# Routing of a top-16 expert layer: candidate rows of eight, and keys found in float16 pairs

## The chip, the cores and the metric

One NeuronCore of a Trainium2 chip runs the whole program; the other seven are idle. The metric is the device time of one execution in microseconds (us), and the kernel before has a median of 2887.47 us over 3 runs (2885.11 to 2893.48). The engines are named as the profile names them: PE (matmul), PEld (weight load), DVE (vector), ACT (scalar), POOL (GpSimd, here the source of gather DMAs), SP (the queue that issues the other DMAs).

## The reference, cut to what matters

The model is two layers. Each has an attention mixer and then a PEER layer: per token and head, two lists of 128 key scores are cut to their best 16, the 16 x 16 sums of the two lists are cut to the best 16, and each of these names one of 16384 experts.

```python
q = (t @ w_q).reshape(b * n, PEER_HEADS, 2, PEER_KEY_DIM)      # 8 heads
s = jnp.einsum('thcd,hcnd->thcn', q, sub_keys)                 # 128 scores per list
sv, si = lax.top_k(s, PEER_TOPK)                               # 16 best of each list
cand = (sv[:, :, 0, :, None] + sv[:, :, 1, None, :]).reshape(b * n, PEER_HEADS, 256)
score, pos = lax.top_k(cand, PEER_TOPK)
i1 = jnp.take_along_axis(si[:, :, 0], pos // PEER_TOPK, axis=-1)
i2 = jnp.take_along_axis(si[:, :, 1], pos % PEER_TOPK, axis=-1)
expert = i1 * PEER_KEYS + i2
gate = jax.nn.softmax(score.astype(jnp.float32), axis=-1)
# then, per token: sum over the 128 chosen experts of gate * gelu(t . u[expert]) * v[expert]
```

Layer 0 does this for 512 tokens (256 of context, 256 of the sequence), layer 1 for the 256 of the sequence.

## The kernel before, in words

A PEER layer computes most tokens densely: a first pass runs over 128 blocks of the table u, and a block multiplies 128 experts with all dense tokens (8 tiles of 128 inputs, and for each three matmuls, since each number is carried as a high and a low float32r part). A second pass does the same with v, after the gelu has been multiplied by a dense weight matrix. The last 128 tokens of layer 0 and the last 32 of layer 1 are done in another way: their experts' rows of u and v are gathered, one row per partition, by POOL's indirect DMA (`fetch`), and DVE multiplies and adds them ("rows", `rows_u` and `rows_v`). So layer 0 has 384 dense tokens and layer 1 has 224.

The routing of a layer runs beside its first pass, in `route`. It has three parts. First 16 steps, one for each head and list: 24 matmuls for the query, a copy by ACT, a score matmul per tile of 128 tokens, and on DVE the 16 best of each list (`top16`: two MAX8, three searches). Then, for each tile of 128 tokens, the sums of the two lists that can be among the best 16 (50 of them, in seven groups `RUNS`), `top16` over these for each of 8 heads, and a one-hot search that finds the expert's number of each chosen place: for two heads at a time a comparison of 2 x 16 x 50 elements with the place (`eq`), a product with the expert numbers, and a sum, all float32 on DVE. The tile with the gathered tokens comes first. Last, `weights`: PE transposes first key, second key and gate of the tile (into `pt`), ACT and DVE copy them as `idx`, and for every 8 tokens DVE makes four one-hot arrays in float16 (tiles `kth`, `ktl`, `qth`, `qtl`), PE multiplies them (32 matmuls of 128 columns), ACT copies the result, and SP writes it to memory (`wd`).

`peer` calls `route` as a generator: each `yield` names a share of work, and after each block of u the routing advances until its sum of shares reaches `(b + 1) * rate`. So the shares and the rate set where the routing's instructions are written between the blocks. The final order on each engine is then made by the tile framework's scheduler before the run, from its own estimates; on the chip each engine runs its list in that order and waits where an input is not there. Two things bend this order. The split of each block of u into high and low part (`split_to`: ACT's cast into `wh`, DVE's subtraction into `wl`, three buffers each) has high priority. And the rows on DVE are held in order behind each other and behind the latest split (`row`, `behind`).

The lines that the change touches are in `route`, the numbers `RUNS` and `NCAND`, one constant tile (`iota`) and the `rate` in `peer`. `self.keys` (named `iota` in the profile, as is the float32 one) holds 0 to 127 in float16, each number twice. In the profile, L990, L993 and L995 are the one-hot search, L963 the sums, L924 to L928 `top16`, L1008 to L1011 the chain that splits an expert's number into its two keys (tiles `ei`, `ef`), L1013 to L1015 the transposes, L1040 to L1043 the one-hot arrays of `weights`, L157 and L158 the two halves of a split, L1121 a row of u, L1098 its gather.

Of the kernel before, what the change touches and what calls it, by code (L numbers as in the profile page):

```python
# [29 lines left out]
PH, TOPK, NK = 8, 16, 128  # L30
# [7 lines left out]
ROUTE_END, LAST = 118, 3  # L38
# [4 lines left out]
RUNS = ((0, 1, 16), (1, 2, 8), (2, 3, 5), (3, 4, 4), (4, 5, 3), (5, 8, 2), (8, 16, 1))  # L43
NCAND = 50
# [82 lines left out]
class Kernel:  # L127
# [125 lines left out]
    def consts(self):  # L253
        nc = self.nc
        jp = self.t([128, 128], I32, "cv")
        nc.gpsimd.iota(jp, pattern=[[1, 128]], base=0, channel_multiplier=-1)
        self.ident = self.t([128, 128], F, "ident")
        nc.vector.tensor_scalar(self.ident, jp, 0.0, None, op0=OP.is_equal)
        self.ones = self.t([128, 128], F, "ones")
        nc.vector.memset(self.ones, 1.0)  # L260
        self.iota = self.t([128, NCAND], F, "iota")
        nc.gpsimd.iota(self.iota, pattern=[[1, NCAND]], base=0, channel_multiplier=0,
                       allow_small_or_imprecise_dtypes=True)
# [666 lines left out]
    def route(self, layer, hh, hl, T, n):  # L930


        nc, a = self.nc, self.a
        nt = T // 128
        sv = self.t([128, nt, 8, 2, TOPK], F, "vh", 2)
        si = self.t([128, nt, 8, 2, TOPK], U32, "vh", 2)
        for hc in range(16):
# [14 lines left out]
            yield 1.0  # L952
        sf = self.t([128, nt, 8, 2, TOPK], F, "vl", 2)
        nc.vector.tensor_copy(sf, si)
        nc.vector.tensor_scalar(sf[:, :, :, 0], sf[:, :, :, 0], 128.0, None, op0=OP.mult)
        for tt in [nt - 1] + list(range(nt - 1)):
            cand = self.t([128, 8, NCAND], F, "kh", 2)
            ec = self.t([128, 8, NCAND], F, "kh", 2)
            o = 0
            for a0, a1, nb in RUNS:  # L960
                na = a1 - a0
                for dst, src in ((cand, sv), (ec, sf)):
                    nc.vector.tensor_tensor(dst[:, :, o:o + na * nb].rearrange("p h (a b) -> p h a b", a=na),  # L963
                                            src[:, tt, :, 0, a0:a1, None].to_broadcast([128, 8, na, nb]),
                                            src[:, tt, :, 1, None, 0:nb].to_broadcast([128, 8, na, nb]), op=OP.add)
                o += na * nb
            yield 1.8
            cv = self.t([128, 8, TOPK], F, "cv")
            cp = self.t([128, 8, TOPK], U32, "cp")
            c2 = self.t([128, 8, NCAND], F, "s2", 5)  # L970
            for h in range(8):
                self.top16(cv[:, h], cp[:, h], cand[:, h], c2[:, h])
                if h % 2:
                    yield 1.2
# [4 lines left out]
            nc.scalar.activation(cv, cv, AF.Exp)  # L979
            nc.vector.tensor_reduce(z, cv, axis=AX, op=OP.add)  # L980
# [3 lines left out]
            cf = self.t([128, 8, TOPK], F, "cf")  # L984
            nc.vector.tensor_copy(cf, cp)
            e = self.t([128, 8, TOPK], F, "e")
# [10 lines left out]
            fl = [x.rearrange("p h j -> p (h j)") for x in (e, cv)]  # L997
            nd = 128
            if tt == nt - 1:
                nd = 128 - n  # L1000
                self.rows_routed(layer, n, *fl)
                self.routed = True
                yield 1.0
            if not nd:
                continue
            ei = self.t([128, 2, 128], I32, "ei")
            ef = self.t([128, 2, 128], F, "ef")
# [7 lines left out]
            nc.tensor.transpose(pT[:, 2], fl[1], self.ident)  # L1015
# [5 lines left out]
            yield 1.8  # L1021
# [120 lines left out]
    def peer(self, layer, hh, hl, T, n, tags, finish, aside=iter(())):  # L1142
# [12 lines left out]
        rate = (16 + T // 128 * 30 + Td / 8 * 2.4) / ROUTE_END  # L1155
# [190 lines left out]
```

## Time and profile before

| | us |
|---|---|
| median of 3 runs | 2887.47 |
| the profiled execution | 2880.45 |
| its span, first to last instruction | 2878.7 |
| PE busy | 2641.1 (92%) |
| DVE busy | 2345.1 (81%) |
| ACT busy | 1271.4 (44%) |
| POOL busy | 492.7 (17%) |

The first pass of layer 0 lies at about 393 to 1093 us of the span, its second pass at 1093 to 1720, the mixer of layer 1 up to about 2000, the first pass of layer 1 at about 2010 to 2505, the second pass to the end. Busy shares are averages over these; a stage has to be looked at by itself. The granted clock of PE has two levels here, 2.4 GHz (1.00) and 1.2 GHz (0.50), and a stretch in between is a mixture.

### The profile page before, as it was taken

The page shows a single profiled execution, that of the slowest core. Times are in us where ns is not written, and L with a number is a line of the kernel's source. Part 1 is how long each engine was busy: PE and PEld are TensorE (multiplying, and loading weights), DVE is VectorE, ACT ScalarE, POOL GpSimd, SP SyncE. Part 2 cuts the span into 40 slices and gives each one's busy share as a digit, 9 for nine tenths or more (in the row PEclk, how much of TensorE's full clock was granted, in tenths as well). Part 3 has the DMA queues.
Part 4 walks back from the last instruction along what each step waited for, and adds up shares of the span by engine and source line. Part 5 has one row for each costly group of instructions (what it writes and reads, how often), then busy time and mean ns, then how long its engine had stood idle before and what let it go on. Part 6 is the DMA issues. An engine that isn't in the chain of part 4 may idle for free. (4 is left out here: it accounts for less than half of the span.)

```text
span 2878.7 us, 44735 instructions
## 1 busy us (share of the span) xinstructions
PE 2641.1 (92%) x16487; PEld 2458.7 (85%) x16487; DVE 2345.1 (81%) x4838; ACT 1271.4 (44%) x1989; POOL 492.7 (17%) x417
## 2 busy tenths in 40 slices
PE   8999989989989899999899998987879899899998
PEld 4788778988979899988899897756879799889998
DVE  7989887998989886978889757876786968668887
ACT  3468532335445453332233333363333556545553
POOL 0113200033323332322333200020000011101000
PEclk9999989999999999999999998968989799999999
DMA  6420433489989899998899854604436699979995
GB/s 225 128 92 16 154 131 110 164 288 317 324 298 338 297 372 332 373 337 318 323 341 387 318 174 137 208 16 139 146 127 238 221 335 316 336 288 357 352 355 170
DMA packets 285278, 712.47 MB, mean 247 GB/s; under 512 B 30209, under 2 KB 130177, under 8 KB 282881
## 3 DMA queue, kind: packets, MB, share of 16 engines
q1 hardware_dynamic: 238978, 541.81, 53.5%
q0 software_dynamic: 46080, 167.79, 16.4%
q8 instruction: 129, 2.11, 0.3%
q14 instruction: 91, 0.75, 0.1%
HBM read 626.64 MB, written 82.84 MB: 246 GB/s over the span
## 5 line engine op out<-in xcount | busy, mean ns | idle before, releaser
L157 ACT CAST wh<-wr 128x1024 fp32r<-128x1024 f32 (+1 forms) x361 | 375.9, 1042 | 813.3 <-PE pa L205 328.9
L158 DVE TENSOR_TENSOR wl<-wr,wh 128x1024 fp32r<-128x1024 f32 (+1 forms) x361 | 436.2, 1209 | 140.2 <-ACT wh L157 139.1
L206 PE MATMUL pa<-A,wl 128*128 128x384 f32 (+1 forms) x1216 | 425.8, 351 | 8.9 <-DVE wl L158 8.9
L205 PE MATMUL pa<-C,wh 128*128 128x384 f32 (+2 forms) x1224 | 427.7, 350 | 0.0
L204 PE MATMUL pa<-A,wh 128*128 128x384 f32 (+1 forms) x1216 | 426.3, 352 | 0.9 <-ACT wh L157 0.9
L206 PE MATMUL pa<-B,wl 128*128 128x224 f32 (+3 forms) x1288 | 379.5, 295 | 41.3 <-DVE wl L158 41.0
L204 PE MATMUL pa<-B,wh 128*128 128x224 f32 (+3 forms) x1288 | 380.3, 297 | 8.5 <-ACT B L404 4.3
L205 PE MATMUL pa<-B,wh 128*128 128x224 f32 (+1 forms) x1216 | 349.9, 288 | 0.2
L206 PEld LDWEIGHTS pa<-B,wl 128*128 128x128 f32 (+1 forms) x1288 | 260.3, 202 | 47.6 <-DVE wl L158 44.0
L1098 POOL DMA_INDIRECT B<-urow,cg x128 | 178.2, 1392 | 557.5 <-DVE B L1121 309.8
L204 PEld LDWEIGHTS pa<-B,wh 128*128 128x128 f32 (+1 forms) x1288 | 260.0, 202 | 14.4 <-ACT B L404 5.1
L157 ACT CAST wh<-pT 128x1024 fp32r<-128x1024 f32 x144 | 151.1, 1050 | 234.0 <-PE pa L205 228.6
L206 PEld LDWEIGHTS pa<-A,wl 128*128 128x128 f32 x1216 | 232.4, 191 | 20.0 <-DVE wl L158 11.8
L205 PEld LDWEIGHTS pa<-B,wh 128*128 128x128 f32 x1216 | 247.0, 203 | 1.2 <-issue 0.5
L205 PEld LDWEIGHTS pa<-C,wh 128*128 128x128 f32 (+1 forms) x1224 | 233.9, 191 | 8.9 <-DVE C L405 0.5
L204 PEld LDWEIGHTS pa<-A,wh 128*128 128x128 f32 x1216 | 232.5, 191 | 9.8 <-ACT wh L157 1.2
L158 DVE TENSOR_TENSOR wl<-pT,wh 128x1024 fp32r<-128x1024 f32 x144 | 175.6, 1221 | 69.7 <-ACT wh L157 68.3
L205 PE MATMUL pa<-pT,wh 128*128 128x384 f32 x512 | 178.7, 349 | 35.2 <-DVE pT L158 34.9
L1121 DVE SCALAR_TENSOR_TENSOR B<-B 128x1024 f32<-128x1024 f32 x128 | 155.4, 1217 | 33.3 <-DMA B<-urow,cg 32.6
L1247 PE MATMUL pa<-pT,wh 128*128 128x448 f32 x512 | 171.5, 378 | 7.1 <-DVE pT L158 4.5
L206 PE MATMUL pa<-pT,wl 128*128 128x384 f32 x512 | 175.5, 343 | 0.0
L204 PE MATMUL pa<-pT,wh 128*128 128x384 f32 x512 | 175.1, 343 | 0.0
(379 smaller groups left out, 6527.3 us busy)
## 6 DMA issues: line engine op xcount, KB each, us to landing
wr<-v SPq DMA_DIRECT2D x152, 512.0 KB
wr<-u SPq DMA_DIRECT2D x128, 512.0 KB
pT<-u SPq DMA_DIRECT2D x128, 512.0 KB
wd<-c SPq DMA_DIRECT2D x38, 1024.0 KB
B<-v SPq DMA_DIRECT2D x72, 512.0 KB
gd<-px SPq DMA_DIRECT2D x64, 384.0 KB
px<-gd SPq DMA_DIRECT2D x63, 384.0 KB
q<-adaw SPq DMA_DIRECT2D x38, 512.0 KB
```

What stands on the lines that cost most here:

```text
L157: nc.scalar.copy(hi, src)
L158: return nc.vector.tensor_tensor(lo, src, hi.bitcast(F), op=OP.subtract)
L204: nc.tensor.matmul(out, lhs[0], rhs[0], start=start, stop=False, **kw)
L205: nc.tensor.matmul(out, lhs[0], rhs[1], start=False, stop=False, **kw)
L206: nc.tensor.matmul(out, lhs[1], rhs[0], start=False, stop=stop, **kw)
L1098: f = self.nc.gpsimd.indirect_dma_start(out=g, out_offset=None, in_=table, in_offset=bass.IndirectOffsetOnAxis(ap=self.eid[:, j:j + 1], ax ...
L1121: self.row(nc.vector.scalar_tensor_tensor(g, g, 1.0, self.own, op0=OP.mult, op1=OP.mult, accum_out=self.act[:, j:j + 1]))
L1247: nc.tensor.matmul(acc[j][:, :2 * Td], v[0][:, s], aa, start=bb == 0, stop=False, skip_group_check=True)
```

## The change

Candidates: instead of 50 sums in seven groups of different width, 80 in ten rows of eight. Rows 0 and 1 are the first entry of the first list with all 16 of the second, rows 2 to 8 are entries 1 to 7 with the first eight, row 9 is entries 8 to 15 with the first one. Row and column of a chosen place are then its number shifted by 3 and its last three bits, and a few operations on 128 elements turn them into the two list positions. The sums are made for four heads at a time, three instructions each.

Keys: for each of the two lists the position is compared with 0 to 15 (not the place with 0 to 49), in float16 and in pairs, for all 8 heads in one instruction of 2048 elements; then the product with the list of keys, and four additions that halve the row each time. The float32 array of expert numbers (`ec`) is gone; the lists are cast once per layer to float16, each entry twice. The two keys come out apart, so the chain L1008 to L1011 is gone; for the gathered tile one instruction joins them.

Shares and rate: the 16 steps count 0.6 instead of 1.0, a tile counts about 20 instead of 30, and the rate follows.

```diff
-NCAND = 50
+NCAND = 80
-            yield 1.0
-        sf = self.t([128, nt, 8, 2, TOPK], F, "vl", 2)
-        nc.vector.tensor_copy(sf, si)
-        nc.vector.tensor_scalar(sf[:, :, :, 0], sf[:, :, :, 0], 128.0, None, op0=OP.mult)
+            yield 0.6
+        lists = self.t([128, nt * 256, 2], H, "vl", 2)
+        nc.vector.tensor_copy(lists, si.rearrange("p t h s j -> p (t h s j)")[:, :, None].to_broadcast([128, nt * 256, 2]))
+        lists = lists.rearrange("p (t h s j) b -> p t h s (j b)", t=nt, h=8, s=2)
+        yield 1.0
...
+            for h0 in (0, 4):
+                cand = self.t([128, 4, NCAND], F, "kh", 2)
+                hs = slice(h0, h0 + 4)
+                for o, a0, na, nb in ((0, 0, 1, 16), (16, 1, 7, 8), (72, 8, 8, 1)):
+                    sh = [128, 4, na, nb]
+                    nc.vector.tensor_tensor(cand[:, :, o:o + na * nb].rearrange("p h (a b) -> p h a b", a=na),
+                                            sv[:, tt, hs, 0, a0:a0 + na, None].to_broadcast(sh),
+                                            sv[:, tt, hs, 1, None, 0:nb].to_broadcast(sh), op=OP.add)
+                c2 = self.t([128, 4, NCAND], F, "s2", 5)
+                for h in range(4):
+                    self.top16(cv[:, h0 + h], cp[:, h0 + h], cand[:, h], c2[:, h])
+                    if h % 2:
+                        yield 2.1
...
+            nc.vector.tensor_scalar(rc[:, 0], fcp.bitcast(I32), 3, None, op0=OP.logical_shift_right)
+            nc.vector.tensor_scalar(rc[:, 1], fcp.bitcast(I32), 7, None, op0=OP.bitwise_and)
+            nc.vector.tensor_copy(rf, rc)
+            r, c = rf[:, 0], rf[:, 1]
...
+            nc.vector.scalar_tensor_tensor(m, r, 9.0, c, op0=OP.is_equal, op1=OP.mult)
+            nc.vector.tensor_tensor(c, c, m, op=OP.subtract)
+            nc.vector.tensor_scalar(ab[:, 0], r, -1.0, 0.0, op0=OP.add, op1=OP.max)
+            nc.vector.tensor_tensor(ab[:, 0], ab[:, 0], m, op=OP.add)
+            nc.vector.tensor_scalar(ab[:, 1], r, 1.0, 8.0, op0=OP.is_equal, op1=OP.mult)
+            nc.vector.tensor_tensor(ab[:, 1], ab[:, 1], c, op=OP.add)
+            yield 2.0
...
-            for h in range(0, 8, 2):
-                eq = self.t([128, 2, TOPK, NCAND], F, "q", 4)
-                sh = [128, 2, TOPK, NCAND]
-                nc.vector.tensor_tensor(eq, self.iota[:, None, None, :].to_broadcast(sh),
-                                        cf[:, h:h + 2, :, None].to_broadcast(sh), op=OP.is_equal)
-                yield 1.75
-                nc.vector.tensor_tensor(eq, eq, ec[:, h:h + 2, None, :].to_broadcast(sh), op=OP.mult)
-                yield 1.75
-                nc.vector.tensor_reduce(e[:, h:h + 2], eq, axis=AX, op=OP.add)
-                yield 1.7
+            ef = self.t([128, 2, 128], F, "ef")
+            for i in range(2):
+                eq = self.t([128, 64, 16, 2], H, "q", 4)
+                nc.vector.tensor_tensor(eq, self.keys[:, None, 0:16].to_broadcast([128, 64, 16, 2]),
+                                        ab[:, i].rearrange("p (g b) -> p g b", b=2)[:, :, None].to_broadcast([128, 64, 16, 2]),
+                                        op=OP.is_equal)
+                yield 1.3
+                e8 = eq.rearrange("p (h k) j b -> p h k (j b)", h=8)
+                nc.vector.tensor_tensor(e8, e8, lists[:, tt, :, i, None].to_broadcast([128, 8, 8, 32]), op=OP.mult)
+                yield 1.3
+                e1 = eq.rearrange("p g j b -> p g (j b)")
+                for w in (16, 8, 4):
+                    nc.vector.tensor_tensor(e1[:, :, 0:w], e1[:, :, 0:w], e1[:, :, w:2 * w], op=OP.add)
+                nc.vector.tensor_tensor(ef[:, i].rearrange("p (g b) -> p g b", b=2), e1[:, :, 0:2], e1[:, :, 2:4], op=OP.add)
+                yield 1.4
...
-            nc.vector.tensor_copy(ei[:, 0], fl[0])
-            nc.vector.tensor_scalar(ei[:, 1], ei[:, 0], 127, None, op0=OP.bitwise_and)
-            nc.vector.tensor_scalar(ei[:, 0], ei[:, 0], 7, None, op0=OP.logical_shift_right)
-            nc.vector.tensor_copy(ef, ei)
...
-        rate = (16 + T // 128 * 30 + Td / 8 * 2.4) / ROUTE_END
+        rate = (16 * 0.6 + T // 128 * 20 + Td / 8 * 2.4) / ROUTE_END
```

The change also moves instructions. The first place is on DVE in layer 0, at the end of the search for the first dense tile: `ef` are the two keys that PE transposes, `B,rg` is a row of u, `wl` a split. Before:

```order
L158 TENSOR_TENSOR wl<-pT,wh 128x1024
L1008 CAST ei<-e 128x128
L1121 SCALAR_TENSOR_TENSOR B,rg<-B 128x1024
L1009 TENSOR_SCALAR ei<-ei 128x128
L1121 SCALAR_TENSOR_TENSOR B,rg<-B 128x1024
L158 TENSOR_TENSOR wl<-pT,wh 128x1024
L1010 TENSOR_SCALAR ei<-ei 128x128
L1121 SCALAR_TENSOR_TENSOR B,rg<-B 128x1024
L1011 CAST ef<-ei 128x256
L1121 SCALAR_TENSOR_TENSOR B,rg<-B 128x1024
L158 TENSOR_TENSOR wl<-wr,wh 128x1024
L1020 SCALAR_TENSOR_TENSOR vl<-pt,vl 128x128
```

The same place now (the lines of the changed file are 11 higher from here on: its row of u is L1132):

```order
L1010 TENSOR_TENSOR ef<-q 128x128
L1009 TENSOR_TENSOR q<-q 128x64x16
L963 TENSOR_TENSOR kh<-vh 128x4x8
L1009 TENSOR_TENSOR q<-q 128x64x8
L1009 TENSOR_TENSOR q<-q 128x64x4
L158 TENSOR_TENSOR wl<-pT,wh 128x1024
L1132 SCALAR_TENSOR_TENSOR B,rg<-B 128x1024
L1010 TENSOR_TENSOR ef<-q 128x128
L158 TENSOR_TENSOR wl<-pT,wh 128x1024
L1132 SCALAR_TENSOR_TENSOR B,rg<-B 128x1024
```

Before, four rows and two splits stand within the chain that makes `ef`, and the reader of the transposes (L1020) follows after one more split; now `ef` is complete six splits ahead of that reader (L1031).

The second place is on DVE in layer 1, in the search for the first tile. Before, from the first comparison on:

```order
L990 TENSOR_TENSOR q<-iota,cf 128x1600
L158 TENSOR_TENSOR wl<-pT,wh 128x1024
L993 TENSOR_TENSOR q<-q,kh 128x1600
L990 TENSOR_TENSOR q<-iota,cf 128x1600
L995 TENSOR_REDUCE e<-q 128x32
L993 TENSOR_TENSOR q<-q,kh 128x1600
L990 TENSOR_TENSOR q<-iota,cf 128x1600
L158 TENSOR_TENSOR wl<-pT,wh 128x1024
```

Now:

```order
L1000 TENSOR_TENSOR q<-iota_69,e 128x2048
L993 TENSOR_REDUCE gz<-cv 128x8
L1005 TENSOR_TENSOR q<-q,vl 128x2048
L994 RECIPROCAL gz<-gz 128x8
L1009 TENSOR_TENSOR q<-q 128x64x16
L995 TENSOR_TENSOR cv<-cv,gz 128x128
L1009 TENSOR_TENSOR q<-q 128x64x8
L1000 TENSOR_TENSOR q<-iota_69,e 128x2048
L1009 TENSOR_TENSOR q<-q 128x64x4
L1005 TENSOR_TENSOR q<-q,vl 128x2048
L158 TENSOR_TENSOR wl<-wr,wh 128x1024
```

Before, the tile's sums, searches and one-hots stand as 103 instructions between six splits in a row (five blocks); now as 80 between four (three blocks).

## Rows read from the trace of the kernel before

**Rows 1.** The page, busy us of each engine, share of the span, instructions.
```profile
PE 2641.1 (92%) x16487; PEld 2458.7 (85%) x16487; DVE 2345.1 (81%) x4838; ACT 1271.4 (44%) x1989; POOL 492.7 (17%) x417
```

**Rows 2.** Windows, first passes: us, busy per engine (instructions), clock, DMA share, GB/s.
```profile
400.00:1093.00 693.00, 655.08 (x4104) 623.61 (x4104) 616.41 (x1489) 304.06 (x386) 176.55 (x127) 0.98 0.79 272
...
2020.00:2500.00 480.00, 433.51 (x3773) 427.35 (x3772) 372.65 (x778) 237.85 (x341) 38.90 (x38) 0.93 0.72 245
```

**Rows 3.** Waits of PE at 400 to 1093: total us, times, longest.
```profile
PE pt L1013 <- DVE ef L1011: 26.2, 3, 10.6
```

**Rows 4.** Timeline of DVE at the third transposes: start, us, instruction [idle before, releaser].
```profile
966.44 0.21 DVE L1008 CAST ei<-e 128x128 int32<-128x128 f32 x1
...
969.95 1.23 DVE L1121 SCALAR_TENSOR_TENSOR B<-B 128x1024 f32<-128x1024 f32 x1 [1.94 <-DMA B<-urow,cg]
...
975.17 1.23 DVE L1121 SCALAR_TENSOR_TENSOR B<-B 128x1024 f32<-128x1024 f32 x1 [3.85 <-DMA B<-urow,cg]
...
977.46 0.28 DVE L1011 CAST ef<-ei 128x256 f32<-128x256 int32 x1
```

**Rows 5.** Windows in layer 0: two around the third transposes, one earlier.
```profile
967.00:977.00 10.00, 0.16 (x1) 0.00 (x0) 4.21 (x9) 0.00 (x0) 2.53 (x4) 0.71 0.86 299
977.00:985.00 8.00, 7.20 (x40) 6.90 (x41) 6.96 (x12) 3.27 (x5) 2.28 (x2) 0.72 0.81 266
...
580.00:610.00 30.00, 25.82 (x138) 24.86 (x138) 28.37 (x76) 10.72 (x14) 10.24 (x7) 0.94 0.81 278
```

**Rows 6.** Timeline of ACT: two casts of blocks of layer 0 that follow each other.
```profile
955.06 1.06 ACT L157 CAST wh<-wr 128x1024 fp32r<-128x1024 f32 x1 [2.72 <-PE pa L205]
...
959.22 1.06 ACT L157 CAST wh<-wr 128x1024 fp32r<-128x1024 f32 x1 [2.72 <-PE pa L205]
```

**Rows 7.** Windows of layer 1, the two stretches of tile routing and one between them.
```profile
2120.00:2170.00 50.00, 33.35 (x208) 32.36 (x207) 46.18 (x149) 13.93 (x20) 2.07 (x2) 0.76 0.29 93
2220.00:2280.00 60.00, 42.90 (x294) 41.47 (x294) 58.83 (x125) 22.87 (x31) 4.38 (x4) 0.72 0.49 150
2170.00:2220.00 50.00, 50.00 (x450) 50.00 (x450) 27.77 (x33) 25.18 (x41) 2.81 (x3) 1.00 0.87 299
```

**Rows 8.** Waits of PE at 2020 to 2500.
```profile
PE pa L206 <- DVE wl L158: 29.8, 9, 5.2
```

**Rows 9.** Lines of DVE by shape at 2127 to 2163: count, busy us, mean ns, idle.
```profile
L990 DVE TENSOR_TENSOR q<-iota,cf 128x1600 f32<-128x1600 f32 x4 | 7.3, 1819 | 0.0
...
L927 DVE MAX8 cv<-s 128x8 f32<-128x50 f32 x8 | 1.7, 207 | 0.0
L928 DVE FIND_INDEX8 cp<-cv,s 128x8 uint32<-128x50 f32 x8 | 1.6, 204 | 0.0
...
L928 DVE MATCH_VALUE_LOAD cp<-cv,s 128x8 f32 x8 | 0.6, 80 | 0.0
...
L963 DVE TENSOR_TENSOR kh<-vl 128x128 f32<-128x128 f32 x2 | 0.6, 287 | 0.0
L928 DVE FIND_INDEX8 vh<-vh,s 128x8 uint32<-128x128 f32 x2 | 0.6, 284 | 0.0
...
L927 DVE MAX8 vh<-s 128x8 f32<-128x128 f32 x1 | 0.3, 283 | 0.0
```

**Rows 10.** Timeline of DVE, two long operations that follow each other.
```profile
2150.79 1.81 DVE L995 TENSOR_REDUCE e<-q 128x32 f32<-128x1600 f32 x1
2152.52 1.81 DVE L993 TENSOR_TENSOR q<-q,kh 128x1600 f32<-128x1600 f32 x1
```

**Rows 11.** Lines of the whole span, the one-hot arrays of the weights in float16.
```profile
L1040 DVE TENSOR_TENSOR kth<-iota,vl 128x1024 f16<-128x1024 f16 x76 | 52.1, 685 | 2.3 <-PE pv L1049 1.8 <-ACT vl L1018 0.5
```

**Rows 12.** Timeline of PE, first and last of eight matmuls of the weights.
```profile
988.18 0.22 PE L1048 MATMUL pv<-kth,qth 128*128 128x128 f16 x1
...
988.59 0.22 PE L1049 MATMUL pv<-kth,qtl 128*128 128x128 f16 x1
```

**Rows 13.** Waits of DVE at 400 to 1093.
```profile
DVE B L1121 <- DMA B<-urow,cg: 28.9, 15, 4.5
```

More of the change, by code (lines that the diff above doesn't have):

```diff
@@ L41 @@
 LAM_INIT = 0.8 - 0.6 * math.exp(-0.3)
-RUNS = ((0, 1, 16), (1, 2, 8), (2, 3, 5), (3, 4, 4), (4, 5, 3), (5, 8, 2), (8, 16, 1))
-NCAND = 50
+NCAND = 80
 def _f(a):
@@ L951, in route @@
                 self.top16(sv[:, tt, hc // 2, hc % 2], si[:, tt, hc // 2, hc % 2], pS[:, tt], s2[:, tt])
-            yield 1.0
-        sf = self.t([128, nt, 8, 2, TOPK], F, "vl", 2)
-        nc.vector.tensor_copy(sf, si)
-        nc.vector.tensor_scalar(sf[:, :, :, 0], sf[:, :, :, 0], 128.0, None, op0=OP.mult)
-        for tt in [nt - 1] + list(range(nt - 1)):
[L957 to L967, printed above, removed]
+            yield 0.6
@@ L968, in route @@
+        lists = self.t([128, nt * 256, 2], H, "vl", 2)
+        nc.vector.tensor_copy(lists, si.rearrange("p t h s j -> p (t h s j)")[:, :, None].to_broadcast([128, nt * 256, 2]))
+        lists = lists.rearrange("p (t h s j) b -> p t h s (j b)", t=nt, h=8, s=2)
+        yield 1.0
+        for tt in [nt - 1] + list(range(nt - 1)):
             cv = self.t([128, 8, TOPK], F, "cv")
             cp = self.t([128, 8, TOPK], U32, "cp")
[L970 to L974, printed above, removed]
+            for h0 in (0, 4):
[11 more added lines that the diff above has]
+                        yield 2.1
@@ L979, in route @@
             nc.scalar.activation(cv, cv, AF.Exp)
+            rc = self.t([128, 2, 128], I32, "ei")
+            fcp = cp.rearrange("p h j -> p (h j)")
+            nc.vector.tensor_scalar(rc[:, 0], fcp.bitcast(I32), 3, None, op0=OP.logical_shift_right)
+            nc.vector.tensor_scalar(rc[:, 1], fcp.bitcast(I32), 7, None, op0=OP.bitwise_and)
+            rf = self.t([128, 2, 128], H, "cf")
+            nc.vector.tensor_copy(rf, rc)
+            r, c = rf[:, 0], rf[:, 1]
+            ab = self.t([128, 2, 128], H, "e")
+            m = self.t([128, 128], H, "m9")
+            nc.vector.scalar_tensor_tensor(m, r, 9.0, c, op0=OP.is_equal, op1=OP.mult)
[5 more added lines that the diff above has]
+            yield 2.0
             nc.vector.tensor_reduce(z, cv, axis=AX, op=OP.add)
@@ L982, in route @@
             nc.vector.tensor_tensor(cv, cv, z[:, :, None].to_broadcast([128, 8, TOPK]), op=OP.mult)
-            cf = self.t([128, 8, TOPK], F, "cf")
-            nc.vector.tensor_copy(cf, cp)
-            e = self.t([128, 8, TOPK], F, "e")
-            for h in range(0, 8, 2):
-                eq = self.t([128, 2, TOPK, NCAND], F, "q", 4)
-                sh = [128, 2, TOPK, NCAND]
-                nc.vector.tensor_tensor(eq, self.iota[:, None, None, :].to_broadcast(sh),
-                                        cf[:, h:h + 2, :, None].to_broadcast(sh), op=OP.is_equal)
-                yield 1.75
-                nc.vector.tensor_tensor(eq, eq, ec[:, h:h + 2, None, :].to_broadcast(sh), op=OP.mult)
-                yield 1.75
-                nc.vector.tensor_reduce(e[:, h:h + 2], eq, axis=AX, op=OP.add)
-                yield 1.7
-            fl = [x.rearrange("p h j -> p (h j)") for x in (e, cv)]
+            ef = self.t([128, 2, 128], F, "ef")
[13 more added lines that the diff above has]
+                yield 1.4
             nd = 128
+            gates = cv.rearrange("p h j -> p (h j)")
             if tt == nt - 1:
                 nd = 128 - n
-                self.rows_routed(layer, n, *fl)
+                e = self.t([128, 128], F, "cp")
+                nc.vector.scalar_tensor_tensor(e, ef[:, 0], 128.0, ef[:, 1], op0=OP.mult, op1=OP.add)
+                self.rows_routed(layer, n, e, gates)
                 self.routed = True
@@ L1014, in route @@
             nc.tensor.transpose(pT[:, 1], ef[:, 1], self.ident)
-            nc.tensor.transpose(pT[:, 2], fl[1], self.ident)
+            nc.tensor.transpose(pT[:, 2], gates, self.ident)
             idx = self.t([128, 4, 128], H, "vl", 2)
@@ L1020, in route @@
             nc.vector.scalar_tensor_tensor(idx[:, 3], pT[:, 2], GSCALE, idx[:, 2], op0=OP.mult, op1=OP.subtract)
-            yield 1.8
+            yield 0.5
             yield from self.weights(tt, nd, idx)
```

5 lines of the change are left out of this document (removed).

## The prediction

> **What bounds the kernel now.** I read the busy shares first, then windows of the two stages that the change touches, then what PE waits for in them, then the timelines at these waits. By the page PE leads with 2641 of 2879 us and DVE follows with 2345 [rows 1]. In the first pass of layer 0 PE is busy 655 of 693 us, in that of layer 1 434 of 480, at clocks of 0.98 and 0.93 [rows 2]. So no more than some 40 to 50 us of idle PE lie in each, plus what the lowered clock costs. DVE work is worth time only where PE waits for it, and there are two kinds of such places.
>
> In layer 0 it is three waits of 26.2 us together: PE stands at the transposes L1013 until DVE has made `ef` [rows 3]. The third one is typical: the chain from L1008 (966.44) to L1011 (977.46) takes 11 us, though its four instructions are short, because rows stand within it and two of these wait 1.94 and 3.85 us for their gathers [rows 4]. PE gets 0.16 us of work into those 10 us, and in the 8 us behind it the clock is at 0.72, so it runs partly at 1.2 GHz [rows 5]. A block of u takes 4.16 us when PE is not held up [rows 6].
>
> In layer 1 it is two stretches in which DVE is the bound: at 2120 to 2170 and 2220 to 2280 DVE is busy 46.2 of 50 and 58.8 of 60 us while PE does 208 and 294 matmuls at clocks of 0.76 and 0.72; between them, with DVE at 28 of 50, PE does 450 in 50 us [rows 7]. At that rate the stretches lack 26.9 us ((450-208)/450 x 50) and 27.3 us (60 - 294/9). PE's waits there are for the split `wl`, 29.8 us in 9 waits [rows 8]: the tile's routing stands between the splits in DVE's list, so the next block comes late. The rest of what is lost is the lower clock.
>
> **The change part by part.** Durations overlap by about 0.08 us: the 1.81 us operations start 1.73 apart [rows 10], so I take 0.08 off each mean.
>
> Removed per tile of 128 tokens: 12 one-hot operations at 1.74 (20.8 us) [rows 9]; `top16` on 50 elements, two MAX8 at 0.13 and three searches at 0.20 (load and search, 0.080 + 0.204 - 0.08), 0.86 per head and 6.8 for eight; 14 sums from 32 to 128 elements, at most 0.21 each and some 2 us in all; the chain L1008 to L1011 and one cast, about 1.0. Together 30.6.
>
> Added per tile: `top16` on 80 elements. Its ends are the rows for 50 (6.8) and for 128 elements (MAX8 0.20, search 0.28: 1.25 per head, 10.0); by elements it lies at 0.4 of the way, 8.0. Six sums of 64, 224 and 32 elements: 128 take 0.21 [rows 9], so about 0.14, 0.30 and 0.10, twice, 1.1. Nine operations on places, 128 to 256 elements, 0.2 each: 1.8. Two comparisons and two products of 2048 float16 elements: the float16 one-hots take 0.605 for 1024 [rows 11], so at most 1.2 each, 4.8. The halving additions of 1024, 512, 256 and 128 elements: 0.6 + 0.33 + 0.2 + 0.2, twice, 2.7. Together 18.4; 12 us less per tile, 73 us over six tiles. Per layer a cast of 2048 or 1024 elements replaces two smaller ones: one more microsecond at most, in the 16 steps, where in layer 0 PE is the bound.
>
> A price that the trace doesn't show is that of float16 with these shapes. It can't be dearer than float32 (1.74 for 1600 elements, 2.2 for 2048), which adds 4 x 1.0 + 2 x 0.95 = 6 us per tile; nor, with two inputs, do rows show anything cheaper than L1040. I take L1040, whose patterns are the same kind (pairs side by side, repeated by a step of zero). The Trainium skill (VectorE: DVE Perf Modes, "What auto-detection actually checks") lets an operation with two inputs run at two elements a cycle only when every tensor is 16-bit with step 1. The trace agrees for L1040: 0.605 us for 1024, against 1.74 for 1600 in float32. By that rule the last addition of each list, which writes float32, has the single rate, which I have charged.
>
> What of it is on the path, layer 1: I count DVE's list. First tile: before, 103 routing instructions (35.7 us at the prices above) and 5 splits (1.14) for five blocks, 41.4 us against 5 x 2.68 of PE (24 matmuls at 450 in 50 us), so 28.0 lost; the window said 26.9. Now 80 instructions (21.2) and 3 splits, 24.6 against 8.0: 16.6 lost, and about 1 us more since some sums now stand before. Gain 10.4. Second tile, with one-hots of the weights in between: before 53.4 us for seven blocks, PE 18.8 and 48 weight matmuls at 0.058 (2.8) [rows 12], 31.8 lost (the window said 27.3; the same count stands on both sides of the difference); now 39.3 for six blocks, 16.1 and 1.8, 21.4 lost. Gain 10.4. Layer 1: **-21**. The clock still falls in these stretches, so nothing is added for it. The 16 steps of layer 1 get 3 blocks fewer between them; PE does these later, no gain or loss.
>
> Layer 0: the waits at the transposes. By count of blocks, PE stood at its three transposes after blocks 36, 67 and 98, and `ef` came after the splits for blocks 38, 70 and 101, so DVE had to be two or three blocks ahead. Now PE reaches them after 28, 61 and 94, and `ef` comes after splits 25, 52 and 85. All three waits go: -26.2, and with them the low clock behind them, about 4 us for the three (0.72 of 8 us is 2.2 us lost at the third, less at the others). Around 580 to 610 PE does 138 matmuls where 173 fit (24 in 4.16), 6 us lost to late splits [rows 5]. There the list was 123.2 us for 28 blocks against 116.5 of PE; now the same work is 89.5 for 22 against 91.5: I take -3, since it is still uneven.
>
> What is late next: the routing of the second and third dense tile now stands among the weights of the tile before. Over the 22 blocks that follow the first transposes DVE's list holds 22 splits (25.1 us), 26 rows at 1.21 (31.5), 64 one-hots at 0.6 (38.4) and 69 routing instructions (17.7), 112.6 us, against 22 x 4.16 + 256 x 0.058 = 106.4 of PE: 6.2 lost, and 5.2 in the same stretch of the next tile. Before, the weight stretches lost 2.9 and 2.6. Net +6. DVE is in order, and a row whose gather is late holds the splits behind it; where DVE has no slack that is paid. The rows wait 28.9 us in 15 waits now [rows 13], a part of it inside the chains. I add +5. Layer 0: -26 - 4 - 3 + 6 + 5 = **-22**.
>
> Nothing outside the first passes moves: mixers and second passes keep their order. Sum -43 against the profiled execution, 2880.45, gives 2837.5; that execution lay 7 us under the median of the runs, so from the median I expect 2887.5 - 43 = 2844.
>
> **The rivals.**
> Layer 0 gives nothing: DVE becomes the bound among the weights and gives the 26 us back there. For it: the two stretches above are already over PE's time. Against: the excess is 11 us by count, not 30. Then only layer 1 counts, 2866.
>
> Float16 runs at the single rate (the rule above, if a zero step counts against the pair): 6 of 12 us per tile are lost. Layer 1 gives 10, layer 0 about 17 since the order of the transposes doesn't depend on it: 2860. Against: L1040.
>
> More: the stretches are smoother than counted, the excess in layer 0 is hidden by the three buffers of `wl` and the 16 steps get shorter too; -60, 2827.
>
> Slower: the rows. They now stand one behind nearly every split, 52 of them in the two dense stretches where DVE has no slack. If every second one waits 2 us for its gather (the mean of the 15 waits), that is 53 us, 2897. It decides from 0.8 us per row on (43/52). Against: 128 rows waited 28.9 us, 0.23 each [rows 13].
>
> No change: DMA stands at 0.87 in the quick stretch of layer 1 [rows 7] and higher later; if transfers then set the pace, time saved early is waited for at the end of the pass. 2887, within its spread.
>
> **How the numbers follow.** Forecast 0.55 (its own range 2832 to 2857), layer 1 alone 0.17, float16 at the single rate 0.08, more 0.07, slower 0.08, no change 0.05. The range for 8 in 10 takes in the first four cases in the main, 2824 to 2878. A difference of 0.3%, 8.7 us, is about what a measurement can tell from none. Faster 0.85 (the first four, less 0.02 for a weak layer 1), within 0.3% 0.07, slower 0.08.
>
> **What would show it.** PE's wait at the transposes in layer 0 falls from 26.2 to under 3 us; in layer 1 PE's waits for `wl` fall from 29.8 to under 20 and two windows with DVE at 95% and a clock near 0.7 remain, shorter; the operations of 2048 elements last 1.2 to 1.3 us; DVE's busy sum falls by 65 to 80 us. If the waits of rows for gathers go far above 28.9 us in layer 0, or PE idles more than 15 us among the weights, the forecast fails by the first or the fourth rival.

## The result and the profile after

The changed kernel takes 2810.27 us (median of 4 runs, 2809.2 to 2813.26) against 2886.72 us for the kernel before (4 runs on the same chip, 2885.11 to 2893.48). The ratio is 0.9732, with an interval of [0.9715, 0.975]: 76 us faster. The forecast was 2844, its range 2824 to 2878, so the time lies outside it. The direction was right and the gain came in the two first passes, where it was said to come; the size was 43 us where 76 came. The profiled execution took 2810.22 us, with a span of 2808.1.

The page's busy line of the kernel after, which answers to [rows 1]:

```profile
PE 2614.9 (93%) x16487; PEld 2440.4 (87%) x16487; DVE 2270.5 (81%) x4818; ACT 1273.5 (45%) x1989; POOL 497.2 (18%) x416
```

DVE has 74.6 us less to do, and the kernel is 76 us shorter. PE does the same 16487 matmuls in 26 us less busy time: a part of the gain is PE's clock.

How the gain divides is read from windows that hold the same blocks. They begin at the first Gelu of a pass and end, in layer 0, at that of block 116 (the last tile's weights are then done), in layer 1 at the last Gelu. By the Gelus the first passes of the kernel before end later than was read from its trace, at 1129 and 2536 us instead of 1093 and 2505, so [rows 2], [rows 8] and [rows 13] leave out their last blocks. Windows of the kernel before (us, busy per engine, clock, DMA share, GB/s):

```profile
396.80:1081.00 684.20, 646.28 (x4062) 614.28 (x4061) 612.89 (x1484) 301.83 (x383) 172.00 (x124) 0.98 0.79 271
...
2025.90:2536.20 510.30, 452.46 (x3944) 445.93 (x3943) 384.61 (x788) 246.97 (x356) 38.90 (x38) 0.93 0.73 248
```

The same blocks in the kernel after:

```profile
393.20:1031.30 638.10, 632.94 (x4061) 606.70 (x4060) 563.65 (x1472) 302.06 (x384) 173.86 (x124) 1.00 0.84 291
...
1979.30:2463.00 483.70, 441.22 (x3944) 435.29 (x3943) 359.12 (x780) 247.82 (x358) 42.08 (x38) 0.96 0.77 261
```

Layer 0 is 46.1 us shorter. PE's idle time (window less busy) falls from 37.9 to 5.2 us, by 32.7; its busy time for practically the same matmuls (4062 and 4061) falls by 13.3 us, as the clock goes from 0.98 to 1.00. Layer 1 is 26.6 us shorter: idle time falls from 57.8 to 42.5 us (15.3), busy time by 11.2, as the clock goes from 0.93 to 0.96. DVE's work in the two windows fell by 49.2 and 25.5 us, nearly the time that each pass gained.

How much of the busy time is the clock can be estimated from the stretches in which it was granted at 0.50. The sums over these stretches: four in layer 0 before, nine in layer 1 before, five in layer 1 after (layer 0 after has none).

```profile
sum 30.60, PE 17.20 PEld 17.21 DVE 23.45 ACT 6.20 POOL 9.22; mean PE 4.30 PEld 4.30 DVE 5.86 ACT 1.55 POOL 2.30
...
sum 68.30, PE 50.88 PEld 50.12 DVE 60.97 ACT 15.08 POOL 4.91; mean PE 5.65 PEld 5.57 DVE 6.77 ACT 1.68 POOL 0.55
...
sum 40.90, PE 27.58 PEld 27.21 DVE 33.33 ACT 15.61 POOL 0.00; mean PE 5.52 PEld 5.44 DVE 6.67 ACT 3.12 POOL 0.00
```

Half of PE's busy time at half the clock is lost: 8.6 us in layer 0, and in layer 1 25.4 before and 13.8 after, a difference of 11.6. So in layer 1 the clock accounts for the 11.2 us of busy time, in layer 0 for some 9 of the 13.3; the rest there stays open.

PE's waits in layer 0's first pass up to block 116, before (us, times, longest), beside the 26.2 us at the transposes in [rows 3]:

```profile
PE pa L206 <- DVE wl L158: 5.7, 6, 2.5
PE pv L1048 <- ACT c L1051: 1.6, 5, 0.6
PE pv L1048 <- DVE qth L1042: 1.6, 1, 1.6
PE pv L1049 <- DVE qtl L1043: 1.6, 3, 0.7
```

The same blocks after:

```profile
PE pv L1059 <- DVE qth L1053: 3.7, 2, 2.3
PE pv L1059 <- ACT c L1062: 0.9, 2, 0.6
PE pa L206 <- DVE wl L158: 0.6, 2, 0.5
```

The transposes don't stand in the list any more, and the waits for splits are nearly gone; those among the weights (tile `pv`) are as before. In layer 1 the split is still waited for. Over the whole pass, before and after:

```profile
PE pa L206 <- DVE wl L158: 39.0, 10, 9.3
...
PE pa L206 <- DVE wl L158: 22.6, 6, 10.3
PE pt L945 <- ACT pc L942: 8.6, 10, 0.9
```

The longest wait of either lies behind block 118, where [rows 8] ends. Against the 29.8 us up to there, the same blocks have after:

```profile
PE pa L206 <- DVE wl L158: 12.3, 5, 4.5
```

DVE's own wait for gathers rose, over all of layer 0's rows before and after ([rows 13] has 124 of the 128):

```profile
DVE B L1121 <- DMA B<-urow,cg: 32.6, 16, 4.5
...
DVE B L1132 <- DMA B<-urow,cg: 48.5, 28, 5.9
```

The new operations, from the lines of DVE at 390 to 1100 by shape (count, busy us, mean ns, idle):

```profile
L1005 DVE TENSOR_TENSOR q<-q,vl 128x2048 f16<-128x2048 f16 x8 | 9.8, 1220 | 0.0
L1000 DVE TENSOR_TENSOR q<-iota,e 128x2048 f16<-128x2048 f16 x8 | 9.8, 1220 | 0.0
...
L1009 DVE TENSOR_TENSOR q<-q 128x1024 f16<-128x1024 f16 x8 | 5.5, 690 | 0.0
...
L1010 DVE TENSOR_TENSOR ef<-q 128x128 f32<-128x128 f16 x8 | 2.3, 290 | 0.0
```

The comparison and the product of 2048 float16 elements last 1.22 us each, as priced.

### The profile page after: what moved, and what is told of

It reads as the page before. It is cut to its first block, busy times and chain, and to the rows that moved or that the text cites. A ratio compares the mean times of both kernels' runs of the same rounds, so it can differ in the third digit from the quotient of the medians.

```text
span 2808.1 us, 44715 instructions
## 1 busy us (share of the span) xinstructions
PE 2614.9 (93%) x16487; PEld 2440.4 (87%) x16487; DVE 2270.5 (81%) x4818; ACT 1273.5 (45%) x1989; POOL 497.2 (18%) x416
## 5 line engine op out<-in xcount | busy, mean ns | idle before, releaser
L206 PE MATMUL pa<-A,wl 128*128 128x384 f32 (+1 forms) x1216 | 418.6, 345 | 4.8 <-DVE wl L158 4.8
L205 PE MATMUL pa<-C,wh 128*128 128x384 f32 (+2 forms) x1224 | 421.8, 346 | 0.0
L206 PE MATMUL pa<-B,wl 128*128 128x224 f32 (+3 forms) x1288 | 373.8, 291 | 24.7 <-DVE wl L158 24.6
L206 PEld LDWEIGHTS pa<-A,wl 128*128 128x128 f32 x1216 | 228.6, 188 | 14.5 <-DVE wl L158 7.0
L205 PE MATMUL pa<-pT,wh 128*128 128x384 f32 x512 | 179.5, 351 | 39.1 <-DVE pT L158 39.0
L1132 DVE SCALAR_TENSOR_TENSOR B<-B 128x1024 f32<-128x1024 f32 x128 | 156.0, 1225 | 49.0 <-DMA B<-urow,cg 48.5
```

The lines of the kernel that those rows point to most:

```text
L205: nc.tensor.matmul(out, lhs[0], rhs[1], start=False, stop=False, **kw)
L206: nc.tensor.matmul(out, lhs[1], rhs[0], start=False, stop=stop, **kw)
L1132: self.row(nc.vector.scalar_tensor_tensor(g, g, 1.0, self.own, op0=OP.mult, op1=OP.mult, accum_out=self.act[:, j:j + 1]))
```

## Experiments

Times are medians, with the ratio to the kernel before on the same chip; its medians lay at 2883 to 2887 us. Block times are from the Gelus of the u blocks.

**One layer at a time.** Each layer chooses the old or the new routing, with that routing's rate:

```
+        new = layer in NEWLAYERS          # (0,) in one kernel, (1,) in the other
-        side = self.route(layer, hh, hl, T, n)
+        side = (self.route if new else self.route_old)(layer, hh, hl, T, n)
```

Layer 0 alone. 

> Layer 0 routed the new way with the new shares and rate, layer 1 the old way. If the two layers add up and layer 0's first pass gains what the changed kernel's trace shows (51 us from the first matmul to the end of the pass, some 8 given back in the second pass): 42 to 48 us less than before, about 2842. If layer 0 is worth only what was forecast (22 us): about 2865. PE's wait at the transposes of layer 0 gone in both.

Measured: 2835.84 us, 0.9841 [0.9805, 0.9877], 48 us faster.

Layer 1 alone. 

> Layer 1 routed the new way with the new shares and rate, layer 0 the old way. By the changed kernel's trace: first pass of layer 1 27 us shorter, time about 2859. By the forecast, 21 us: 2866. The waits at the transposes of layer 0 stay at 26 us.

Measured: 2858.05 us, 0.9904 [0.9873, 0.9934], 26 us faster. 48 and 26 make 74 of the 76 us: the layers add up. The forecast had 22 and 21, so most of what was missing lies in layer 0.

**Only the order at the transposes.** The kernel before, all its DVE work kept, with the transposes further back in PE's order, where `ef` comes before them; a greater rate packs the rest:

```
             nc.vector.tensor_copy(ef, ei)
+            if layer == 0:
+                yield 14.0
...
+        rate = (16 + T // 128 * 30 + Td / 8 * 2.4 + (42 if layer == 0 else 0)) / ROUTE_END
```

> The kernel before, except that in layer 0 the transposes of the keys stand some blocks of u later in the program (one more yield, rate adapted); all arithmetic of the search stays, so DVE has as much to do as before. If the three waits at the transposes cost about 15 us each, with the low clock and the restart behind them, and that is nearly all of layer 0's gain: 35 to 45 us less, about 2847. If only the idle 26 us and a little clock hang on them (the forecast's 30) and the rest of layer 0's 46 us came from less DVE work: 20 to 30 us less, about 2862. If the waits only move to the next reader: no change.

Measured: 2887.24 us, 1.0012 [0.9996, 1.0027]: nothing, the third of the three expectations. Its waits of PE in layer 0:

```profile
PE pa L206 <- DVE wl L158: 20.2, 9, 5.8
PE pv L1050 <- DVE qth L1044: 15.7, 3, 8.7
PE pv L1050 <- ACT c L1053: 2.5, 4, 1.8
PE pt L1015 <- DVE ef L1011: 1.5, 1, 1.5
```

The 26.2 us at the transposes are down to 1.5, but PE now waits for the one-hots of the weights and for the splits. Blocks 12 to 116 took 544.0 us against 538.2. Here the wait named the place where DVE's lateness showed, and moving the reader moved the wait. The run changes two things at once, though: the greater rate also writes all of layer 0's routing into fewer blocks. So it shows that this other order gains nothing, not that no order does.

**Less DVE work in the old algorithm.** The kernel before with one-hots over the first 25 of 50 candidates (keys of the others are left out):

```
-                sh = [128, 2, TOPK, NCAND]
+                half = NCAND // 2
...
+                sh = [128, 2, TOPK, half]
```

> The kernel before, its 12 one-hot operations per tile over 25 of the 50 candidates only (keys of places 25 to 49 are left out of the result); search, sums in float32, chain and yields as before. It takes about 12 x 0.85 = 10 us of DVE per tile away, nearly as much as the change (12). Theory now: it is DVE's work between the splits that layer 0 and layer 1 pay for, whatever the algorithm, so most of the 76 us comes: some 2825 (2815 to 2835). Rival (the chain into the transposes, four operations with rows between them, or the wider rows of eight): the old chain still stands there, layer 0 keeps its waits of 10 us each, only layer 1 gains: 2865 (2858 to 2872).

Measured: 2827.84 us, 0.9807 [0.9784, 0.983], 56 us faster, for 59.4 us less of DVE (page: 2285.7). Window from the first Gelu to that of block 116:

```profile
397.40:1037.10 639.70, 634.32 (x4055) 609.41 (x4054) 574.61 (x1484) 301.81 (x383) 166.12 (x124) 0.99 0.83 289
```

Layer 0's pass is practically that of the changed kernel (639.7 against 638.1 us) with the four-operation chain, the sums and the searches of before. Layer 1's pass took 493.7 us, against 510.4 before and 483.6 in the changed kernel. Less work also let the order bring `ef` earlier (after the splits for blocks 28, 61 and 92, ahead of the transposes behind 34, 66 and 98), so this run alone does not part work from order. Beside the run above, where later transposes gave nothing, work is the likelier cause; less work in an unchanged order was not run.

**The work put back.** Ten multiplications of 1024 elements per tile that nobody reads, first ahead of the sums:

```
                 hs = slice(h0, h0 + 4)
+                for _ in range(5):
+                    load = self.t([128, 1024], F, "q", 4)
+                    one = sv[:, tt, 0, 0, 0:1].to_broadcast([128, 1024])
+                    nc.vector.tensor_tensor(load, one, one, op=OP.mult)
```

> The changed kernel with ten additional multiplications of 1024 float32 elements per tile ahead of its sums, whose results nobody reads: about 11 us of DVE per tile, what the change had taken away; chain, one-hots and yields stay. Theory (work): layer 0 loses some 40 again and layer 1 some 20, 2865 to 2880, with PE waiting for DVE in layer 0 by 20 us or more and a clock under 1.00 in some windows. Rival (chain or order of the last operations before the transposes): in layer 0 the load falls where PE has blocks enough, only layer 1 loses: 2825 to 2835, clock 1.00 throughout layer 0's first pass.

Measured: 2849.49 us, 0.9881 [0.9854, 0.9909]. Half of the gain is gone, between the two expectations. These operations depend on nothing late, and DVE's order spreads them well ahead of the routing that follows. So the same work was then bound to the one-hots, with `one = ab[:, i, 0:1]...` between comparison and product:

> The changed kernel with ten additional multiplications of 1024 elements per tile, whose results nobody reads, now placed between comparison and product of the two one-hots and fed from the places, so that they can't run ahead: about 11 us of DVE per tile where the old one-hots stood. In the run with the load ahead of the sums half of the 76 us came back (2849). Theory (DVE's work, counted where it stands against PE's blocks): nearly all comes back, 2876 (2865 to 2890), with 20 us or more of PE waits at layer 0's transposes and a clock under 1.00 there. Rival (half of the gain is the algorithm's itself, shorter last steps and other order, wherever the load stands): 2850 (2843 to 2857).

Measured: 2865.39 us, 0.9939 [0.9917, 0.9961]: 55 of 76 us gone, again between the two. PE's waits in layer 0 are those of the kernel before, smaller:

```profile
PE pt L1029 <- DVE ef L1014: 13.6, 2, 8.4
PE pa L206 <- DVE wl L158: 5.9, 4, 3.3
PE pt L1028 <- DVE ef L1014: 4.2, 1, 4.2
```

Two loads of the same size (40 operations in layer 0 and 20 in layer 1, 1.22 us each; by the page 64 and 67 us of DVE) cost 39 and 55 us, 0.6 and 0.8 of their time: where work stands decides what share of it is paid.

**The two halves of the change.** The changed kernel with its 16 places, its one-hots in float32, each list in two halves:

```
+                for g in (0, 32):
...
-                eq = self.t([128, 64, 16, 2], H, "q", 4)
+                    eq = self.t([128, 32, 16, 2], F, "q", 4)
```

> The changed kernel with its 16 places, but comparisons, products and additions in float32 (each list in two halves, results unchanged). By the rows 2048 float32 elements take some 2.2 instead of 1.2 us and the additions about twice their time: 6 us of DVE per tile more, half of what the change had saved. Theory (work, in proportion): half of the gain is lost, 2845 (2835 to 2856). Rival (DVE has slack left in the changed kernel, only what goes beyond it costs): 2818 (2812 to 2828).

Measured: 2846.59 us, 0.9843 [0.9808, 0.9879]. About half of the gain goes with the narrower type, the rest with the shorter lists and places (the four runs spread from 2832 to 2851). Its products, from the lines of DVE:

```profile
L1006 DVE TENSOR_TENSOR q<-q,vl 128x1024 f32<-128x1024 f32 x16 | 19.5, 1217 | 0.0
```

2048 elements take 2.43 us in two float32 operations, against 1.22 in one of float16.

**The chain.** The changed kernel with the old four operations (cast, split up, cast) between the last addition and the transposes, and for the dense tiles one more that joins the two keys first:

```
+            if tt != nt - 1:
...
+                nc.vector.scalar_tensor_tensor(e, ef[:, 0], 128.0, ef[:, 1], op0=OP.mult, op1=OP.add)
...
+            nc.vector.tensor_copy(ei[:, 0], e)
+            nc.vector.tensor_scalar(ei[:, 1], ei[:, 0], 127, None, op0=OP.bitwise_and)
+            nc.vector.tensor_scalar(ei[:, 0], ei[:, 0], 7, None, op0=OP.logical_shift_right)
+            nc.vector.tensor_copy(ef, ei)
```

> The changed kernel with the old chain of four operations (pack, split up again, cast) put back between the last addition and the transposes: 2 us of DVE per tile at the most, but the dependent chain that the transposes waited for. Theory (work): 2810 to 2818. Rival (chain): the waits at layer 0's transposes are back, 2835 or more, with 15 us or more of them in the trace.

Measured: 2819.44 us, 0.9779 [0.974, 0.9819], 9 us more for 7 us more of DVE, though its four runs spread from 2813 to 2832, and no wait at the transposes in layer 0. In the changed kernel the chain held nothing up.

**The clock.** The kernel before with 45 matmuls of 256 columns that nobody needs ahead of each of layer 0's transposes:

```
+            if layer == 0:
+                for _ in range(45):
+                    nc.tensor.matmul(pT[:, 0:2]..., self.keys[:, :, 0], self.keys..., start=True, stop=True)
             nc.tensor.transpose(pT[:, 0], ef[:, 0], self.ident)
```

> The kernel before with 45 matmuls of 256 float16 columns (about 4.8 us by the rate of the u blocks) ahead of each of layer 0's three transposes, into the tile that these overwrite: PE works there while it would wait for the indices; routing is unchanged. It tells what the lowered clock behind the waits costs, 13 us by the busy sums of the two traces (646 us at 0.98 against 633 at 1.00 for the same 4061 matmuls). Theory: most of the clock loss goes at no price, 2876 (2870 to 2882), with the clock nearer to 1.00 around 640 to 660, 810 to 830 and 970 to 990. Rival (the matmuls are paid in full, the clock falls all the same, or the cost is the idling alone): 2887 to 2900.

Measured: 2881.36 us, 0.9975 [0.996, 0.9989]: 5 us faster though PE has 135 matmuls more to do. By the profiled execution (2889 us, the slowest of the ten), windows of 50 us at the waits:

```profile
640.00:690.00 50.00, 43.22 (x309) 41.69 (x310) 42.35 (x75) 25.25 (x32) 13.91 (x11) 0.93 0.81 278
...
790.00:840.00 50.00, 43.67 (x298) 41.65 (x297) 45.13 (x84) 18.81 (x25) 13.86 (x12) 0.93 0.79 268
...
940.00:990.00 50.00, 45.22 (x289) 43.77 (x288) 41.52 (x58) 19.94 (x27) 16.92 (x12) 0.97 0.84 299
```

The same windows of the kernel before:

```profile
640.00:690.00 50.00, 41.13 (x291) 37.97 (x290) 41.96 (x67) 23.74 (x30) 16.12 (x12) 0.93 0.86 293
...
790.00:840.00 50.00, 39.71 (x251) 37.20 (x250) 41.12 (x59) 19.38 (x26) 14.03 (x12) 0.90 0.77 260
...
940.00:990.00 50.00, 39.09 (x236) 38.18 (x235) 42.74 (x56) 16.74 (x22) 16.71 (x11) 0.90 0.84 288
```

The filling was too short for the longest waits (9.1 us of wait at the transposes were left), the clock fell less in two of the three places, and the kernel gained 5 us. It supports the clock's part without settling its size. It isn't clean either: the matmuls moved PE's order by a block.

**A better version.** The changed kernel with sums, searches and one-hots held behind the split that was issued last, so that they spread between the splits:

```
+    def after_split(self, ins):
+        if self.layer == 1:                # the first of the two runs: without this line
+            self.behind(ins, self.paced)
...
-                    self.top16(cv[:, h0 + h], cp[:, h0 + h], cand[:, h], c2[:, h])
+                    self.after_split(self.top16(cv[:, h0 + h], cp[:, h0 + h], cand[:, h], c2[:, h]))
```

Both layers. 

> The changed kernel, except that each sum, search and one-hot operation of a tile's routing is held in DVE's order behind the latest split of u, so that the routing spreads over the blocks as it is written. If what is left to lose in layer 1 are the two packed stretches of routing (about 12 and 17 us beyond 2.67 us per block in the trace after): 18 to 28 us less than the changed kernel, about 2787. If the 16 steps or the transfers set the pace there: 2805 to 2812. In layer 0, where the keys now come 0 to 1 blocks ahead of the transposes instead of 3 to 9, the waits at the transposes could come back: then up to 30 us more, 2820 to 2840.

Measured: 2799.24 us, 0.9702 [0.9675, 0.9728]. In layer 1 the first pass was 19 us shorter than in the changed kernel; in layer 0 the blocks to 116 took 6 us more, with a wait of 4.3 us at a transpose. The time lies between the three expectations: the gain in layer 1 came as hoped, layer 0 lost less than feared.

Layer 1 alone. 

> The changed kernel with its sums, searches and one-hots held behind the split that was issued last (as in the run with all of them held), in layer 1 alone. In that run layer 1's first pass was 19 us shorter and layer 0's 6 us longer than in the changed kernel. If the layers are independent: 2810 - 19 = 2792 (2788 to 2797), below the run with both, 2799. Rival (the 19 us came from a start that layer 0 had delayed): 2800 to 2810.

Measured: 2795.31 us, 0.9687 [0.9662, 0.9711], below the kernel before and the changed one by intervals that don't overlap, but not told apart from the run with both layers ([0.9675, 0.9728]). Layer 1's first pass is as short as there (466.0 and 465.0 us), so its gain doesn't come from layer 0:

```profile
1982.30:2448.30 466.00, 433.67 (x3944) 428.59 (x3943) 359.87 (x780) 247.55 (x357) 45.66 (x38) 0.98 0.80 271
```

DVE's work is that of the changed kernel (359.87 against 359.12), the pass 17.7 us shorter: idle 32.3 instead of 42.5, busy 433.7 instead of 441.2.

**Work on DVE elsewhere.** The changed kernel with a multiplication of 512 elements per block in layer 0's second pass:

```
+            if layer == 0:
+                load = self.t([128, 512], F, "kth", 2)
+                one = A[:, 0:1].to_broadcast([128, 512])
+                nc.vector.tensor_tensor(load, one, one, op=OP.mult)
```

> The changed kernel with one additional multiplication of 512 float32 elements per block of layer 0's second pass (128 of them, about 0.6 us each, 77 us of DVE), whose results nobody reads; the first passes and the routing stay. DVE's work there was 83% of the stretch. Theory (a microsecond of DVE costs a microsecond of the kernel where the routing stands, in bursts between the splits, but spread evenly over a stretch it costs little): 2826 (2812 to 2845). Rival (any work on DVE costs its time, since PE hangs on the splits everywhere): 2880 (2865 to 2895).

Measured: 2788.27 us, 0.9671 [0.9653, 0.9689]: some 22 us faster than the changed kernel with 72 us more on DVE. Both expectations failed. Layer 1's first Gelu came at 1956.4 instead of 1979.3, though layer 0's first pass began 3.2 us later: that pass took 678.8 instead of 684.5 us from first to last Gelu, and the second pass 574.7 instead of 595.1. The second pass got quicker though it had more to do: the additional work also changed the order. The second pass of the changed kernel and of this one:

```profile
1076.70:1671.80 595.10, 555.97 (x3077) 548.82 (x3076) 474.61 (x604) 188.90 (x257) 155.51 (x122) 0.97 0.87 324
...
1074.20:1648.90 574.70, 546.04 (x3077) 532.74 (x3077) 545.35 (x730) 193.66 (x257) 215.44 (x122) 1.00 0.90 337
```

For the same matmuls PE idled 28.7 instead of 39.1 us and was busy for 9.9 us less, as the clock went from 0.97 to 1.00, so half of the gain there is PE's busy time. PE's and DVE's waits, changed kernel, 1043 to 1645:

```profile
PE pa L205 <- DVE pT L158: 39.0, 19, 4.9
...
DVE s L297 <- DMA q<-adaw: 47.6, 11, 7.0
DVE s L1238 <- DMA px<-gd: 38.8, 15, 7.3
```

And with the load:

```profile
PE pa L205 <- DVE pT L158: 17.0, 19, 1.7
PE pa L204 <- ACT pT L157: 10.9, 9, 1.4
...
DVE s L1238 <- DMA px<-gd: 11.8, 5, 3.7
```

The operations on `adaw` (L297) no longer wait for their loads at all, and PE's waits are short ones now. That it is this order, and not another part of the shift, was not isolated.

## Why the prediction was right in direction and wrong in size

DVE's busy time and the kernel's time, over the runs that change the routing's work:

| kernel | DVE busy | median |
|---|---|---|
| before | 2345.1 | 2886.72 |
| load at the one-hots | 2337.8 | 2865.39 |
| load ahead of the sums | 2334.8 | 2849.49 |
| layer 1 new | 2317.5 | 2858.05 |
| one-hots in float32 | 2311.9 | 2846.59 |
| layer 0 new | 2296.1 | 2835.84 |
| half the one-hots | 2285.7 | 2827.84 |
| old chain | 2277.5 | 2819.44 |
| after | 2270.5 | 2810.27 |

Apart from the two loads, each lies within 7 us of the line from the first row to the last (76 us for 75 of DVE). The loads cost less, 14 and 27 us under that line. So the work that the change took out was paid practically in full where it stood. That is a finding on these places, not on DVE's total: the two kernels with the routing held behind the splits (2799 and 2795 us at 2273 and 2271 of DVE) and the one with work in the second pass (2788 at 2343) lie 13, 16 and 96 us under the line.

1. **The price of the operations** was right: 73 us less was the sum, 74.6 the page. The comparisons and products did not fall to the single rate, so that rival is out.
2. **The waits at the transposes** all went, as said. But the reason given (the transposes come late enough, so the wait is won) was not sufficient: in the kernel before, moving them back took the wait away (26.2 to 1.5 us) and left the time. In the changed kernel the wait could be won because the work that made it had gone too; so far the term of -26 was right by luck.
3. **What is late next, +6 and +5**, is the step that failed. I took DVE to be the bound among the weights, counted what its list exceeds PE's blocks by as lost, and added waits for gathers. PE's waits among the weights were 4.8 us before and 4.6 after: the two terms came to nothing. In the window in which DVE has least slack, the kernel after shows:

```profile
640.00:690.00 50.00, 50.00 (x372) 48.74 (x371) 48.81 (x126) 29.31 (x36) 20.98 (x12) 1.00 1.00 349
```

DVE is at 98%, and PE isn't held up at all. The 22 blocks behind the first transposes took 110.1 us, 3.7 over PE's 106.4 by the prediction's own count. The gathers did delay DVE more (32.6 to 48.5 us), but all of PE's idle time up to block 116 was 5.2 us. The waits for splits, which I let fall by 3, fell by 5.1. So by idle time layer 0 won 32.7 us where the terms had -26 - 3 + 6 + 5 = -18.
4. **The clock, -4**, was the second term that was mis-sized: PE's busy time in layer 0 fell by 13.3 us, of which some 9 are the clock by the stretches at 0.50 and the rest is open. In layer 1 I had added nothing for it, since the clock would still fall; by the windows 11.2 of its 26.6 us are PE's busy time. The windows at one wait [rows 5] showed only the 8 us directly behind it. Windows of 50 us of the kernel before would have shown 0.97, 0.93, 0.90, 0.90 and 0.97 at five places of layer 0's first pass; in the kernel after all lie at 1.00 there.
5. **Layer 1, -21**: the window gives -26.6. The stretches of the two tiles gained 14.1 and 14.5 us instead of 10.4 each. The places were right, two stretches with a lower clock do remain, and over the blocks of [rows 8] the waits for `wl` fell to 12.3 us, under the 20 that were said. Windows of the kernel after:

```profile
2075.00:2125.00 50.00, 42.16 (x325) 41.71 (x324) 32.59 (x79) 19.86 (x31) 4.06 (x3) 0.83 0.61 211
2125.00:2175.00 50.00, 38.60 (x322) 37.41 (x322) 44.50 (x126) 24.14 (x35) 2.81 (x3) 0.90 0.57 182
2175.00:2225.00 50.00, 50.00 (x500) 49.83 (x499) 44.84 (x59) 33.08 (x45) 8.37 (x7) 1.00 1.01 350
```

In the first of them DVE is busy for only 33 of 50 us (against 46 in [rows 7]), because the stretch is shorter now than the window. Cut in two:

```profile
2075.00:2094.00 19.00, 11.16 (x56) 10.71 (x55) 18.79 (x68) 5.28 (x8) 0.00 (x0) 0.61 0.21 69
2094.00:2125.00 31.00, 31.00 (x270) 31.00 (x270) 13.79 (x12) 14.57 (x23) 4.06 (x3) 0.97 0.86 298
```

Up to 2094 the routing still fills DVE and holds PE up; behind it PE is busy throughout.
6. **Rivals.** DMA did not take the gain back: both first passes are shorter by about what DVE's work in them fell by. The rows' gathers, the rival on the other side, got later and were not paid in layer 0, so their rise, named as a sign of being wrong, pointed the wrong way. The nearest was "more", 2827, which had 0.07; a part of its reason (the excess among the weights is hidden) is what the window at 640 to 690 shows.

Put in one sum: of 73 us of DVE work I let 43 count and 30 fall into slack; by the table it counted practically in full. The windows have 72.7 us, some 30 more than the terms: 14.7 are idle time of layer 0, 9.3 its busy time beyond the 4 for the clock, 5.6 layer 1.

## What to carry to other kernels

Where an engine in order feeds PE and PE's waits for it turn up at several readers, price the work taken from that engine at its full duration first, and subtract slack only where a window shows PE at work and the feeder idle. Read idle time and PE's busy time for the same count of matmuls apart: the second holds the clock, and it was 24.5 of 73 us here, some 20 of them the clock by the stretches at 0.50. Before explaining a wait by the chain in front of it, move the reader; if the wait turns up elsewhere and the time stays, the reader's place was not the cause.

## What the runs showed that I had not expected

Where DVE's work stands was worth nearly as much as how much there is: in layer 1 the order alone gave 17.7 us, where the change gave 26.6.

More work on DVE came with a faster kernel, where operations that had waited 47.6 us for loads no longer did and PE's mean clock there rose from 0.97 to 1.00; which of the shifts in the order did it is open. In layer 0's first pass, where DVE waited as long for gathers (48.5 us), PE was idle for 5.2 us in all.

A float16 comparison of 2048 elements with both inputs repeated by steps of zero, and a product with one of them so repeated, took 1.22 us each; two float32 products of 1024 took 2.43 together.
